# Three more pairs of the down projection in the seven-product form, their weight sums made during gate and up, and a written order for the loads

## The chip, the core and the metric

The kernel runs on one core of one Trainium2 chip. The metric is the device time of one execution in microseconds (us). TensorE (PE in the profile) multiplies matrices, VectorE (DVE) and ScalarE (ACT) work elementwise, GpSimd (POOL) here does little but issue transfers, and SyncE (SP) issues nearly all loads. Each engine takes its instructions in the order of its own queue. On-chip memory is named by tiles; a tile that is declared with `bufs=n` has n places that are used in turn, so whoever writes place k again waits for the last reader of what it held.

## What is computed

One decoder layer in float32 on 256 tokens of width 2048. The change lies in its last part:

```python
x = x + concat(PoolMixer, MLA, MemXAttn) @ W_o
h = rms_norm(x, g_ffn)
g = h @ w_gate                                   # 2048 x 5632
gc = conv_b + sum_j conv_w[j] * shifted(g, j)    # causal, width 3
x = x + (silu(gc) * (h @ w_up)) @ w_down         # w_down: 5632 x 2048
```

## The kernel before

**Precision.** Every float32 operand is split in two parts of a shorter type: a high part `wh` (ACT, `nc.scalar.copy`) and the rest `wl` (DVE, the operand minus its high part). A product takes three matmuls: high times high, low times high, high times low. `split_w` (L95) does this for weights. It writes into the tiles `wh` and `wl`, four places each of 128x1024, so at most four split blocks exist at a time.

**Gate and up** (loop at L879, 43 turns after the first). Turn f loads a block of 128x2048 of `w_g` and one of `w_u` into the staging tile `wr` (three places), splits each, and `gemm_pair` (L154) runs 96 matmuls with 256 columns. `glu` (L824) then makes 128 rows of the activation: convolution, SiLU, product, and its split. Two turns (f even, then odd) make one pair j of 256 rows; there are 22 pairs.

**Down** (loop at L988) goes twice over the 22 pairs, once for each half c of the output columns. For a pair and a half, the activation (256 tokens by 256 rows) and the weights (256 rows by 1024 columns, 1 MiB) are each seen as 2x2 blocks. Three kinds of pair exist; the string `KIND` (L43) has a letter for each place in `ORDER` (L42):

- `p`, plain (`plain`, L912): 8 block products, 24 matmuls with 512 columns. The weights are split in two pieces of 1024.
- `S` and `s`, seven products (`seven`, L940): 7 block products, 21 matmuls. They need sums of the blocks of the activation (seven blocks with high and low part: tile `aS`, made in `glu`, kept until down), and sums of the blocks of the weights. Split are one piece of 512 (`b11`) and three of 1024 (`b2`, then `t13` and `t24` from the sums).
- For `s`, DVE makes the weight sums in down (`make_sums`, L928), ahead of the pair: the instructions stand in the middle of the pair before it, where `seven` and `plain` call `between`. For `S`, they were made ahead of time: `presum` (L859) runs in odd turns of gate and up, loads the block through the same staging tile `wr`, makes four subtractions of 128x512 on DVE, and writes 1 MiB to a tensor in device memory, `tsum`. In down, `seven` then loads 0.75 MiB of the block and 1 MiB of `tsum`.

Before, 14 of 22 pairs take seven products; 8 of these are `S`, so 16 sums are made in gate and up.

**What sets the order.** A scheduler orders each engine's queue by what it expects to be ready, except for instructions marked by `keep` (L91), which stay in the order in which they are written. In down nearly everything on ACT, DVE and PE is kept; in gate and up nothing is, the loads on SP included. Loads of down (`load_dn`, L897) use four places in turn: three of `wr` and one in the tile `dn`.

Of the kernel before, what the change touches and what calls it, by code (L numbers as in the profile page):

```python
# [18 lines left out]
P = 128  # L19
# [22 lines left out]
ORDER = tuple(range(PAIRS - 3)) + (PAIRS - 1, PAIRS - 2, PAIRS - 3)  # L42
KIND = "pSspSsSpsSpSspSsSpsSpp"  # L43
# [20 lines left out]
def layer(ctx, tc, xT_d, xn_d, memT_d, vec_d, tab_d, w_z_d, w_mqkr_d, w_q_d, w_kv_d, w_mem_d, w_pool_d, w_o_d,  # L64
# [759 lines left out]
    def glu(f, psg, psu, home=None):  # L824
# [34 lines left out]
    def presum(i):  # L859

        raw = load_w(w_dn_d[SUMMED[i]], STG)
        r = raw.rearrange("p (b n) -> p b n", n=NN)
        for d, a, b in ((0, 1, 0), (1, 2, 1), (2, 2, 0), (3, 3, 2)):
            nc.vector.tensor_tensor(r[:, d], r[:, a], r[:, b], op=ALU.subtract)  # L864
# [30 lines left out]
    cnt = [0, 0]  # L895

    def load_dn(src, parts=((0, STG),)):  # L897

        cnt[1] += 1
        raw = dn[:, 4:8].rearrange("p b n -> p (b n)") if cnt[1] % 4 == 0 else stage.tile(  # L900
            [P, STG], F32, tag="wr", name=nm("wr"), bufs=3)[:]
        for a, b in parts:
            nc.sync.dma_start(raw[:, a:b], src[:, a:b])
        return raw
# [7 lines left out]
    def plain(c, j, own, first, last, kept, between=None, by_bank=False):  # L912
# [8 lines left out]
        for k, t, n in order:  # L921
            a = [aT[j][:, k, o + t * P:o + (t + 1) * P] for o in (0, T)]
            s = n if k == 0 else 1 - n
            prod(own[t, n], a, [w[:, s * NN:(s + 1) * NN] for w in ws[k]], first and k == 0, last and k == 1)

    ready = {}

    def make_sums(c, j):  # L928

        raw = load_dn(w_dn_d[c, j])  # L930
        r3 = raw.rearrange("p (b n) -> p b n", n=NN)
        i = cnt[0] % 2
        cnt[0] += 1
        f13, f24 = dn[:, 2 * i:2 * i + 2], dn[:, 2 - 2 * i:4 - 2 * i]
        keep(nc.vector.tensor_tensor(f13, r3[:, 1:3], r3[:, 0:2], op=ALU.subtract))
        keep(nc.vector.tensor_tensor(f24[:, 0], r3[:, 2], f13[:, 0], op=ALU.subtract))
        keep(nc.vector.tensor_tensor(f24[:, 1], r3[:, 3], f24[:, 0], op=ALU.subtract))
        ready[c, j] = (raw, *(f.rearrange("p b n -> p (b n)") for f in (f13, f24)))

    def seven(c, j, own, com, first, last, kept, between):  # L940
        if (c, j) in SUMMED:
            raw = load_dn(w_dn_d[c, j], ((0, NN), (2 * NN, STG)))
            sums = load_dn(tsum[:, SUMMED.index((c, j))])
            F13, F24 = sums[:, 0:HS], sums[:, HS:STG]
        else:
            raw, F13, F24 = ready.pop((c, j))
        b11 = split_w(raw, 0, NN, kept=kept)
# [3 lines left out]
        t13 = split_w(F13, 0, HS, kept=kept)  # L951
        t24 = split_w(F24, 0, HS, kept=kept)
        for (b, s), f, ps, own_ in (((b11, 0), 6, com[0], False), ((b2, 0), 5, own[0, 1], True),
                                    ((b2, 1), 0, own[0, 0], True), ((t13, 0), 2, com[1], False),
                                    ((t13, 1), 4, com[3], False), ((t24, 0), 3, com[2], False),
# [57 lines left out]
def _pack(**i):  # L1013
# [61 lines left out]
    w = np.stack([w[:, 0, :, :, 0], w[:, 0, :, :, 1], w[:, 1, :, :, 1], w[:, 1, :, :, 0]])  # L1075
# [19 lines left out]
```

## Time and profile before

| | |
|---|---|
| median of 3 runs | 996.81 us (996.54 to 997.71) |
| the profiled execution | 996.77 us, of which 994.8 us are its span |
| granted TensorE clock | 1.000 over the whole span |
| PE busy | 988.6 us |
| DVE busy / ACT busy | 756.8 us / 566.2 us |
| moved by DMA | 246.51 MB, mean 248 GB/s |
| gate and up, from the first of its matmuls at L165 | 301.7 to 769.8 us |
| down | 769.8 to 990.6 us |

The span runs from the first to the last instruction; the time of the execution has about 2 us around it. Busy shares are averages over stages with different limits. Matmuls overlap one another, so the length that the profile gives for one matmul is longer than the distance from its start to the next one's; distances between starts are what the PE queue costs.

### The profile page before, as it was taken

How to read it: one execution, taken by the hardware profiler on the slowest of the kernel's cores; microseconds unless marked ns; L12 is line 12 of the kernel's file. 1: busy time of each engine (PE TensorE's matmuls, PEld its weight loads, DVE VectorE, ACT ScalarE, POOL GpSimd, SP SyncE). 2: the span in 40 equal slices, each digit the busy share in tenths (PEclk: the TensorE clock that was granted, in tenths of full speed). 3: DMA queues.
4: the chain of work that ended last, by engine and by line, in shares of the span. 5: the costliest groups of instructions: out<-in, count | busy, mean ns of one | idle time of the engine just before them, and what ended most of it. 6: DMA issues, size and time to landing. Idle time of an engine off the chain costs nothing.

```text
span 994.8 us, 17144 instructions
## 1 busy us (share of the span) xinstructions
PE 988.6 (99%) x6888; PEld 916.3 (92%) x6888; DVE 756.8 (76%) x1117; ACT 566.2 (57%) x770; POOL 31.2 (3%) x63
## 2 busy tenths in 40 slices
PE   9999999999999999999999999999999999999998
PEld 7899988888889999999999999999999888888886
DVE  6878588765676777777787777876666988899897
ACT  6777666644565554554554455455544666746663
POOL 1100000000000000000000000000000000000000
PEclk9999999999999999999999999999999999999999
DMA  9867445344665888877788887775656887879772
GB/s 358 299 240 292 137 157 182 124 145 143 211 220 189 300 290 298 300 274 290 276 300 294 299 309 266 289 277 189 203 185 203 297 282 265 288 270 313 297 256 105
DMA packets 43808, 246.51 MB, mean 248 GB/s; under 512 B 4944, under 2 KB 5456, under 8 KB 19792
## 3 DMA queue, kind: packets, MB, share of 16 engines
q1 hardware_dynamic: 36576, 220.50, 63.1%
q0 software_dynamic: 6720, 24.12, 6.3%
q8 instruction: 54, 0.88, 0.3%
q10 hardware_dynamic: 432, 0.79, 0.3%
q14 instruction: 26, 0.21, 0.1%
HBM read 224.42 MB, written 20.97 MB: 247 GB/s over the span
## 4 chain that ended last, share of the span: by engine, by line
PE 96%; DVE 2%; DMA 1%; ACT 1%; issue 0%; DVEq 0%; ACTq 0%
PE psm L165 47%; PE psm L181 5%; PE psm L183 5%; PE psm L182 5%; PE psm L148 4%; PE psm L910 4%; PE psm L908 4%; PE psm L909 4%; PE psa L908 3%; PE psa L909 3%; PE psa L910 3%; PE psm L132 2%; PE psa L713 1%; PE psa L181 1%; PE psa L183 1%; PE psa L182 1%
## 5 line engine op out<-in xcount | busy, mean ns | idle before, releaser
L102 DVE TENSOR_TENSOR wl<-wr,wh 128x1024 fp32r<-128x1024 f32 (+2 forms) x362 | 419.1, 1168 | 166.9 <-ACT wh L101 110.1
L101 ACT CAST wh<-wr 128x1024 fp32r<-128x1024 f32 (+2 forms) x362 | 362.6, 1007 | 201.3 <-PE psm L165 84.7
L165 PE MATMUL psm<-h,wh 128*128 128x256 f32 x2752 | 319.1, 276 | 0.0
L165 PEld LDWEIGHTS psm<-h,wh 128*128 128x128 f32 x2752 | 315.3, 188 | 0.0
L165 PE MATMUL psm<-h,wl 128*128 128x256 f32 x1376 | 162.9, 276 | 0.0
L165 PEld LDWEIGHTS psm<-h,wl 128*128 128x128 f32 x1376 | 159.2, 188 | 0.0
L101 ACT CAST wh<-dn 128x1024 fp32r<-128x1024 f32 (+1 forms) x54 | 52.7, 976 | 32.2 <-PE psa L909 17.9
L102 DVE TENSOR_TENSOR wl<-dn,wh 128x1024 fp32r<-128x1024 f32 (+1 forms) x54 | 59.7, 1122 | 8.8 <-ACT wh L101 6.7
L828 ACT ACTIVATE gc<-g,vec 128x256 f32<-128x256 f32 x44 | 26.5, 603 | 70.0 <-DVE g L826 70.0
L831 ACT ACTIVATE gc<-gc 128x256 f32<-128x256 f32 x44 | 18.4, 419 | 70.5 <-DVE gc L830 70.4
L864 DVE TENSOR_TENSOR wr<-wr 128x512 f32<-128x512 f32 x64 | 44.0, 688 | 1.1
L830 DVE SCALAR_TENSOR_TENSOR gc<-g,vec,gc 128x255 f32<-128x255 f32 x88 | 42.2, 479 | 1.0
L910 PE MATMUL psm<-wl,aS 128*128 128x512 f32 x98 | 38.2, 390 | 0.1
L908 PE MATMUL psm<-wh,aS 128*128 128x512 f32 x98 | 38.1, 389 | 0.0
L910 PE MATMUL psa<-wl,aS 128*128 128x512 f32 x98 | 38.1, 389 | 0.0
L908 PE MATMUL psa<-wh,aS 128*128 128x512 f32 x98 | 38.1, 389 | 0.0
L909 PE MATMUL psa<-wh,aS 128*128 128x512 f32 x98 | 38.1, 389 | 0.0
L909 PE MATMUL psm<-wh,aS 128*128 128x512 f32 x98 | 38.1, 389 | 0.0
L181 PE MATMUL psm<-wh,cat 128*128 128x512 f32 x96 | 38.1, 397 | 0.0
L183 PE MATMUL psm<-wl,cat 128*128 128x512 f32 x96 | 37.4, 390 | 0.0
L182 PE MATMUL psm<-wh,cat 128*128 128x512 f32 x96 | 37.4, 389 | 0.0
L866 POOL DMA_DIRECT2D tsum<-wr x32 | 17.0, 533 | 344.5 <-DVE wr L864 344.5
(232 smaller groups left out, 1355.0 us busy)
## 6 DMA issues: line engine op xcount, KB each, us to landing
wr<-in_w_g SPq DMA_DIRECT2D x44, 1024.0 KB, 5.1
wr<-in_w_u SPq DMA_DIRECT2D x44, 1024.0 KB, 5.6
wr<-in_w_dn SPq DMA_DIRECT2D x37, 1024.0 KB, 5.0
wr<-in_w_o SPq DMA_DIRECT2D x16, 1024.0 KB, 4.9
tsum<-wr POOLq DMA_DIRECT2D x32, 512.0 KB, 4.1
wr<-tsum SPq DMA_DIRECT2D x12, 1024.0 KB, 6.2
wr<-in_w_z SPq DMA_DIRECT2D x10, 1024.0 KB, 6.8
dn<-in_w_dn SPq DMA_DIRECT2D x7, 1024.0 KB, 6.5
```

The source lines that it names most:

```text
L101: keep(nc.scalar.copy(hi[:, c:e], raw[:, o + c:o + e]), kept)
L102: keep(nc.vector.tensor_tensor(lo[:, c:e], raw[:, o + c:o + e], hi[:, c:e].bitcast(F32), op=ALU.subtract), kept)
L148: keep(nc.tensor.matmul(ps, parts[k // nk][low][:, i * P:(i + 1) * P], m, start=k + a == 0 and low == low_first, stop=k == KD - 1 and low ...
L165: nc.tensor.matmul(ps, parts[k // nk][low][:, i * P:(i + 1) * P], m, start=k + a == 0 and low == (s == 1), stop=k == KD - 1 and low == (s ...
L181: keep(nc.tensor.matmul(ps, xh, hi[:, i, o], start=first and i == 0, stop=False), kept)
L182: keep(nc.tensor.matmul(ps, xl, hi[:, i, o], start=False, stop=False), kept)
L183: keep(nc.tensor.matmul(ps, xh, lo[:, i, o], start=False, stop=last and i == nk - 1), kept)
L830: nc.vector.scalar_tensor_tensor(gc[:, d:T], g[:, 0:T - d], v(w, f), gc[:, d:T], op0=ALU.mult, op1=ALU.add)
L864: nc.vector.tensor_tensor(r[:, d], r[:, a], r[:, b], op=ALU.subtract)
L908: nc.tensor.matmul(ps, a[0], b[0], start=first, stop=False)
L909: nc.tensor.matmul(ps, a[1], b[0], start=False, stop=False)
L910: nc.tensor.matmul(ps, a[0], b[1], start=False, stop=last)
```

## The change

It does five things.

1. `KIND` and `ORDER`: 17 of 22 pairs take seven products, 14 of them as `S` (28 sums made in gate and up) and 3 as `s`.
2. The sums get their own staging tile `wj` with two places. Their loads (`job_load`) and the loads of gate and up are marked `keep`, so that SP's queue has them as written: after the two loads of a turn. The subtractions (`job_sums`) are written one turn later. A dictionary `job_at` spreads 28 jobs over the turns 2 to 41.
3. Five activations (`AWAY`, pairs 16 to 20) do not stay on the chip: they are written to `forms` in device memory and read back in each half of down into a single place `aL` (`fetch`, on POOL's queue, issued when the pair that used the place before is done).
4. In down the loads use six places in turn: three of `wr`, two of `wj`, one in `dn`.
5. The columns of the stored weight blocks are arranged so that an `S` pair's load is one transfer, and `make_sums` is four subtractions of 128x512 instead of one of 128x1024 and two of 128x512.

```diff
-ORDER = tuple(range(PAIRS - 3)) + (PAIRS - 1, PAIRS - 2, PAIRS - 3)
-KIND = "pSspSsSpsSpSspSsSpsSpp"
+KIND = "pSSSsSSpSSsSSpSsSSSSpp"
+ORDER = (0, 1, 16, 2, 3, 4, 17, 5, 21, 6, 18, 7, 8, 9, 19, 10, 11, 12, 20, 13, 14, 15)
+AWAY = (16, 17, 18, 19, 20)
...
-    def load_w(src, n, cut=STG):
+    def load_w(src, n, cut=STG, kept=False):
         raw = stage.tile([P, STG], F32, tag="wr", name=nm("wr"), bufs=3)
         for c in range(0, n, cut):
-            nc.sync.dma_start(raw[:, c:min(n, c + cut)], src[:, c:min(n, c + cut)])
+            keep(nc.sync.dma_start(raw[:, c:min(n, c + cut)], src[:, c:min(n, c + cut)]), kept)
...
-            aT[j] = home if j == PAIRS - 1 else fp.tile([P, 14, P], F32R, name=nm("aS"))[:]
+            aT[j] = (home if j == PAIRS - 1 else away() if j in AWAY
+                     else fp.tile([P, 14, P], F32R, name=nm("aS"))[:])
...
+            if j in AWAY:
+                nc.gpsimd.dma_start(forms[:, AWAY.index(j)], aT[j])
+    forms = dp.tile([P, len(AWAY), 14, P], F32R, name="forms")
+    def away():
+        return fp.tile([P, 14, P], F32R, tag="aL", name=nm("aL"), bufs=1)[:]
     tsum = dp.tile([P, len(SUMMED), STG], F32, name="tsum")
-    def presum(i):
-        raw = load_w(w_dn_d[SUMMED[i]], STG)
+    def job_place():
+        return fp.tile([P, STG], F32, tag="wj", name=nm("wj"), bufs=2)[:]
+    def job_load(i):
+        raw = job_place()
+        keep(nc.sync.dma_start(raw, w_dn_d[SUMMED[i]]))
+        return i, raw
+    def job_sums(i, raw):
         r = raw.rearrange("p (b n) -> p b n", n=NN)
-        for d, a, b in ((0, 1, 0), (1, 2, 1), (2, 2, 0), (3, 3, 2)):
+        for d, a, b in ((1, 0, 1), (0, 2, 0), (2, 2, 1), (3, 3, 2)):
             nc.vector.tensor_tensor(r[:, d], r[:, a], r[:, b], op=ALU.subtract)
...
+    job_at = {2 + i * (KF - 5) // (len(SUMMED) - 1): i for i in range(len(SUMMED))}
+    job = None
...
-        gemm_pair(pss, [load_w(w[f], STG) for w in (w_g_d, w_u_d)], h2)
+        gemm_pair(pss, [load_w(w[f], STG, kept=True) for w in (w_g_d, w_u_d)], h2)
         if f < KF - 1:
             glu(f, *pss)
-        if f % 2 and 3 <= f < 3 + 2 * len(SUMMED):
-            presum(f // 2 - 1)
+        if job is not None:
+            job_sums(*job)
+        job = job_load(job_at[f]) if f in job_at else None
...
-    def load_dn(src, parts=((0, STG),)):
-        cnt[1] += 1
-        raw = dn[:, 4:8].rearrange("p b n -> p (b n)") if cnt[1] % 4 == 0 else stage.tile(
-            [P, STG], F32, tag="wr", name=nm("wr"), bufs=3)[:]
-        for a, b in parts:
-            nc.sync.dma_start(raw[:, a:b], src[:, a:b])
+    def load_dn(src, a=0):
+        cnt[0] += 1
+        n = cnt[0] % 6
+        raw = (dn[:, 4:8].rearrange("p b n -> p (b n)") if n == 0 else job_place() if n % 3 == 1
+               else stage.tile([P, STG], F32, tag="wr", name=nm("wr"), bufs=3)[:])
+        nc.sync.dma_start(raw[:, a:STG], src[:, a:STG])
         return raw
...
+    def fetch(j):
+        aT[j] = away()
+        nc.gpsimd.dma_start(aT[j], forms[:, AWAY.index(j)])
...
     def make_sums(c, j):
         raw = load_dn(w_dn_d[c, j])
-        r3 = raw.rearrange("p (b n) -> p b n", n=NN)
-        i = cnt[0] % 2
-        cnt[0] += 1
-        f13, f24 = dn[:, 2 * i:2 * i + 2], dn[:, 2 - 2 * i:4 - 2 * i]
-        keep(nc.vector.tensor_tensor(f13, r3[:, 1:3], r3[:, 0:2], op=ALU.subtract))
-        keep(nc.vector.tensor_tensor(f24[:, 0], r3[:, 2], f13[:, 0], op=ALU.subtract))
-        keep(nc.vector.tensor_tensor(f24[:, 1], r3[:, 3], f24[:, 0], op=ALU.subtract))
-        ready[c, j] = (raw, *(f.rearrange("p b n -> p (b n)") for f in (f13, f24)))
+        r = raw.rearrange("p (b n) -> p b n", n=NN)
+        for d, a, b in ((1, r[:, 0], r[:, 1]), (0, r[:, 2], r[:, 0]), (2, r[:, 2], dn[:, 1]), (3, r[:, 3], dn[:, 2])):
+            keep(nc.vector.tensor_tensor(dn[:, d], a, b, op=ALU.subtract))
+        ready[c, j] = (raw, dn[:, 0:4].rearrange("p b n -> p (b n)"))
...
+        rest = [j for j in ORDER if j in AWAY]
+        fetch(rest.pop(0))
...
                 seven(c, j, own, com, j == SEVEN[0], j == SEVEN[-1], kept, between)
+                if j in AWAY and rest:
+                    fetch(rest.pop(0))
```

The letters stand under one another so:

```
before  pSspSsSpsSpSspSsSpsSpp
after   pSSSsSSpSSsSSpSsSSSSpp
```

**First place: DVE in down, the sums of an `s` pair.** DVE's queue before, at the sums for the pair at place 12 of the first half; `wl` with a `wh` is a split (512 wide: `b11`; then `b2`; after the sums `t13` and `t24`), `dn<-` are the sums. The pair at place 10, ahead of these rows' `S` pair, is plain: its two splits come first.

```order
L102 TENSOR_TENSOR wl_9202<-wr_9199,wh_9201 128x1024
L102 TENSOR_TENSOR wl_9206<-wr_9199,wh_9205 128x1024
L102 TENSOR_TENSOR wl_9238<-dn,wh_9237 128x512
L102 TENSOR_TENSOR wl_9242<-dn,wh_9241 128x1024
L935 TENSOR_TENSOR dn<-wr_9245 128x1024
L936 TENSOR_TENSOR dn<-wr_9245,dn 128x512
L937 TENSOR_TENSOR dn<-wr_9245,dn 128x512
L102 TENSOR_TENSOR wl_9251<-wr_9235,wh_9250 128x1024
L102 TENSOR_TENSOR wl_9255<-wr_9235,wh_9254 128x1024
```

DVE's queue of the change at the sums for the pair at place 10 of the first half:

```order
L103 TENSOR_TENSOR wl_9242<-wr_9237,wh_9241 128x512
L103 TENSOR_TENSOR wl_9246<-wr_9237,wh_9245 128x1024
L103 TENSOR_TENSOR wl_9250<-wr_9239,wh_9249 128x1024
L103 TENSOR_TENSOR wl_9254<-wr_9239,wh_9253 128x1024
L103 TENSOR_TENSOR wl_9283<-wj_9278,wh_9282 128x512
L103 TENSOR_TENSOR wl_9287<-wj_9278,wh_9286 128x1024
L959 TENSOR_TENSOR dn<-dn 128x512 x4
L103 TENSOR_TENSOR wl_9296<-wr_9280,wh_9295 128x1024
L103 TENSOR_TENSOR wl_9300<-wr_9280,wh_9299 128x1024
```

In both, the sums stand between `b2` and the first split of the sums; what has changed is the pair ahead: four splits of an `S` pair now, two of a plain pair before. It is so at places 4 and 10 of each half. At place 15 the `S` pair that carries the sums still follows a plain one.

**Second place: ACT at the start of gate and up.** ACT's queue before, from the square root of the normalization to the SiLU of turn 0 (`ACTIVATE gc<-gc`); `wh_3108` and `wh_3112` are the high parts of turn 1's `w_g`:

```order
L208 ACTIVATE rc<-rc,eps 128x2
L101 CAST wh_3108<-wr_3104 128x1024
L101 CAST wh_3112<-wr_3104 128x1024
L193 ACTIVATE h_2547<-psa_3002,vec 128x256
L193 ACTIVATE h_2547<-psa_3007,vec 128x256
L193 ACTIVATE h_2547<-psa_3012,vec 128x256
L193 ACTIVATE h_2547<-psa_3017,vec 128x256
L815 COPY r_2938<-psa_3028 128x256
L101 CAST wh_3164<-wr_3106 128x1024
L828 ACTIVATE gc_3093<-g_3091,vec 128x256
L101 CAST wh_3168<-wr_3106 128x1024
```

ACT's queue of the change from the same instruction:

```order
L209 ACTIVATE rc<-rc,eps 128x2
L194 ACTIVATE h_2547<-psa_3003,vec 128x256
L194 ACTIVATE h_2547<-psa_3008,vec 128x256
L194 ACTIVATE h_2547<-psa_3013,vec 128x256
L194 ACTIVATE h_2547<-psa_3018,vec 128x256
L816 COPY r_2938<-psa_3029 128x256
L829 ACTIVATE gc_3094<-g_3092,vec 128x256
L832 ACT_TABLE_LOAD
L832 ACTIVATE gc_3094<-gc_3094 128x256
L102 CAST wh_3109<-wr_3105 128x1024
L191 CAST aT_3099<-gc_3094 128x256
L102 CAST wh_3113<-wr_3105 128x1024
```

The casts of turn 1's `w_g` stand behind the SiLU of turn 0 now; on DVE the `wl` of the same block stands behind `glu`'s last product of turn 0 in the same way.

**Third place: SP in gate and up.** SP's queue of the change from turn 1 on:

```order
L89 DMA wr_3105<-in_w_g 128x2048
L89 DMA wr_3107<-in_w_u 128x2048
L89 DMA wr_3233<-in_w_g 128x2048
L89 DMA wr_3235<-in_w_u 128x2048
L874 DMA wj_3359<-in_w_dn 128x2048
L89 DMA wr_3363<-in_w_g 128x2048
L89 DMA wr_3365<-in_w_u 128x2048
L874 DMA wj_3499<-in_w_dn 128x2048
L89 DMA wr_3503<-in_w_g 128x2048
L89 DMA wr_3505<-in_w_u 128x2048
```

A load for sums stood in `wr` in every second turn before; it stands in `wj` in two of three turns now, with no place of `wr` taken.

More of the change, by code (lines that the diff above doesn't have):

```diff
@@ L922, in plain @@
             a = [aT[j][:, k, o + t * P:o + (t + 1) * P] for o in (0, T)]
-            s = n if k == 0 else 1 - n
+            s = 1 - n
             prod(own[t, n], a, [w[:, s * NN:(s + 1) * NN] for w in ws[k]], first and k == 0, last and k == 1)
+    def fetch(j):
+        aT[j] = away()
+        nc.gpsimd.dma_start(aT[j], forms[:, AWAY.index(j)])
     ready = {}
@@ L930, in make_sums @@
         raw = load_dn(w_dn_d[c, j])
-        r3 = raw.rearrange("p (b n) -> p b n", n=NN)
-        i = cnt[0] % 2
-        cnt[0] += 1
-        f13, f24 = dn[:, 2 * i:2 * i + 2], dn[:, 2 - 2 * i:4 - 2 * i]
-        keep(nc.vector.tensor_tensor(f13, r3[:, 1:3], r3[:, 0:2], op=ALU.subtract))
-        keep(nc.vector.tensor_tensor(f24[:, 0], r3[:, 2], f13[:, 0], op=ALU.subtract))
-        keep(nc.vector.tensor_tensor(f24[:, 1], r3[:, 3], f24[:, 0], op=ALU.subtract))
-        ready[c, j] = (raw, *(f.rearrange("p b n -> p (b n)") for f in (f13, f24)))
+        r = raw.rearrange("p (b n) -> p b n", n=NN)
+        for d, a, b in ((1, r[:, 0], r[:, 1]), (0, r[:, 2], r[:, 0]), (2, r[:, 2], dn[:, 1]), (3, r[:, 3], dn[:, 2])):
+            keep(nc.vector.tensor_tensor(dn[:, d], a, b, op=ALU.subtract))
+        ready[c, j] = (raw, dn[:, 0:4].rearrange("p b n -> p (b n)"))
     def seven(c, j, own, com, first, last, kept, between):
         if (c, j) in SUMMED:
-            raw = load_dn(w_dn_d[c, j], ((0, NN), (2 * NN, STG)))
+            raw = load_dn(w_dn_d[c, j], NN)
             sums = load_dn(tsum[:, SUMMED.index((c, j))])
-            F13, F24 = sums[:, 0:HS], sums[:, HS:STG]
         else:
-            raw, F13, F24 = ready.pop((c, j))
-        b11 = split_w(raw, 0, NN, kept=kept)
+            raw, sums = ready.pop((c, j))
+        b11 = split_w(raw, NN, NN, kept=kept)
         b2 = split_w(raw, 2 * NN, HS, kept=kept)
@@ L950, in seven @@
             between()
-        t13 = split_w(F13, 0, HS, kept=kept)
-        t24 = split_w(F24, 0, HS, kept=kept)
+        t31 = split_w(sums, 0, HS, kept=kept)
+        t24 = split_w(sums, HS, HS, kept=kept)
         for (b, s), f, ps, own_ in (((b11, 0), 6, com[0], False), ((b2, 0), 5, own[0, 1], True),
-                                    ((b2, 1), 0, own[0, 0], True), ((t13, 0), 2, com[1], False),
-                                    ((t13, 1), 4, com[3], False), ((t24, 0), 3, com[2], False),
+                                    ((b2, 1), 0, own[0, 0], True), ((t31, 1), 2, com[1], False),
+                                    ((t31, 0), 4, com[3], False), ((t24, 0), 3, com[2], False),
                                     ((t24, 1), 1, own[1, 0], True)):
@@ L1074, in _pack @@
     w = a["w_down"][0].reshape(PAIRS, 2, P, 2, 2, NN)
-    w = np.stack([w[:, 0, :, :, 0], w[:, 0, :, :, 1], w[:, 1, :, :, 1], w[:, 1, :, :, 0]])
+    w = np.stack([w[:, 0, :, :, 1], w[:, 0, :, :, 0], w[:, 1, :, :, 1], w[:, 1, :, :, 0]])
     r["w_dn"] = w.transpose(3, 1, 2, 0, 4).reshape(2, PAIRS, P, STG)
```

2 lines of the change are left out of this document (1 added, 1 removed).

## The prediction

> **What bounds the kernel now.** I read the page first: its busy times and its chain of waits.
>
> ```profile
> span 994.8 us, 17144 instructions
> PE 988.6 (99%) x6888; PEld 916.3 (92%) x6888; DVE 756.8 (76%) x1117; ACT 566.2 (57%) x770; POOL 31.2 (3%) x63
> PE 96%; DVE 2%; DMA 1%; ACT 1%; issue 0%; DVEq 0%; ACTq 0%
> ```
>
> PE is busy for 988.6 of 994.8 us, and the chain is PE's own queue for 96%. The 6 us left lie at the two ends, so no wait inside can be removed for a gain: only fewer matmuls make it faster, and every wait that is added on PE makes it longer. So two things are to be reckoned: the matmuls that go, and where PE starts to wait.
>
> What a matmul costs is read from the timeline of PE in down: the start of a plain pair (operand `aT`), of the seven-product pair behind it (`aS`), and of the pair after that.
>
> ```profile
> 804.31 0.39 PE L908 MATMUL psa<-wh,aT 128*128 128x512 f32 x1
> 809.75 0.39 PE L908 MATMUL psm<-wh,aS 128*128 128x512 f32 x1
> 814.51 0.39 PE L908 MATMUL psm<-wh,aS 128*128 128x512 f32 x1
> ```
>
> A plain pair takes 5.44 us for 24 matmuls, a seven-product pair 4.76 us for 21: 0.2267 us from start to start, back to back.
>
> **What goes: 4.1 us.** Three pairs change from plain to seven products, in two halves: 6 x 3 = 18 matmuls x 0.2267 = 4.08 us. Down becomes 954 x 0.2267 = 216.3 us.
>
> **What comes, 1: the sums of an `s` pair now meet full split buffers.** The next rows are ACT's, DVE's and PE's timeline: a seven-product pair that starts at 799.55, its split of `b2`, and then the one place of down where PE waits (827.48), with the sums ahead of it.
>
> ```profile
> 798.16 1.06 ACT L101 CAST wh<-wr 128x1024 fp32r<-128x1024 f32 x1 [0.30 <-PE psm L909]
> 797.89 2.59 DVE L102 TENSOR_TENSOR wl<-wr,wh 128x1024 fp32r<-128x1024 f32 x2 [0.21 <-ACT wh L101]
> 799.55 0.39 PE L908 MATMUL psm<-wh,aS 128*128 128x512 f32 x1
> ...
> 823.61 1.23 DVE L935 TENSOR_TENSOR dn<-wr 128x1024 f32<-128x1024 f32 x1 [2.06 <-DMA wr<-in_w_dn]
> 824.87 0.69 DVE L936 TENSOR_TENSOR dn<-wr,dn 128x512 f32<-128x512 f32 x1
> 825.60 0.69 DVE L937 TENSOR_TENSOR dn<-wr,dn 128x512 f32<-128x512 f32 x1
> 826.21 2.35 DVE L102 TENSOR_TENSOR wl<-wr,wh 128x1024 fp32r<-128x1024 f32 x2
> ...
> 826.97 0.39 PE L909 MATMUL psm<-wh,aS 128*128 128x512 f32 x1
> 827.48 0.50 PE L910 MATMUL psm<-wl,aS 128*128 128x512 f32 x1
> 827.82 0.40 PE L908 MATMUL psm<-wh,aS 128*128 128x512 f32 x1
> ...
> L910 PE MATMUL psm<-wl,aS 128*128 128x512 f32 x98 | 38.2, 390 | 0.1
> ```
>
> ACT's cast waits for PE (L909): the four places of `wh` are full, and a split can only be as far ahead as one seven-product pair. So in a row of such pairs the split of `b2` starts 1.66 us before its pair does (797.89 against 799.55). Another 1024-wide split may start 1.14 us later (two take 2.59 with a gap; 826.21 has two in 2.35, so 2.35 - 1.22 = 1.13). The first split of the sums is needed by the third matmul of its products, 9 + 2 = 11 matmuls or 2.49 us after the pair's start.
>
> Behind a plain pair there is more room: that pair has only two split tiles, so the next pair's `b2` finds its place a pair earlier. That is where all seven-product carriers of sums stand in the rows of before, and PE waits only once (the group's row has 0.1 us of idle time in all, the modelled ends hide the rest), where the sums' load was 2.06 us late. This one place shows the chain as it is: the split of 826.21 ends at 827.44, and the matmul that should have started at 827.20 starts at 827.48; the next starts at 827.82 instead of 827.43. That wait, 0.4 us, goes, as its pattern goes.
>
> At places 4 and 10 of each half the carrier now follows another seven-product pair. The time from the pair's start: `b2` at -1.66, sums from -0.52, 2.6 us (823.61 to 826.21; the new form, four of 512, has starts 0.6 to 0.73 apart, about the same), first split of the sums 2.08 to 3.31, where PE needs it at 2.49. That is 0.86 us, and 0.1 us is lost in starting again, as after 827.48. I take 0.9 us x 4 places = **3.7 us**. Below, it is nothing, if PE were a microsecond late there anyway; above, 2.6 us each, if nothing of the sums were hidden: 0 to 10 us. The third `s` pair, place 15, still sits behind a plain pair: nothing.
>
> **What comes, 2: the first turn of gate and up.** Rows of DVE, ACT and PE around 300 us:
>
> ```profile
> 298.36 1.10 PE L132 MATMUL psm<-h,wl 128*128 128x256 f32 x8
> 299.31 1.58 PE L132 MATMUL psm<-h,wh 128*128 128x256 f32 x12
> 300.72 1.10 PE L132 MATMUL psm<-h,wl 128*128 128x256 f32 x8
> 301.66 0.28 PE L165 MATMUL psm<-h,wh 128*128 128x256 f32 x1
> ...
> 299.56 0.42 DVE L826 TENSOR_TENSOR g<-psm,r 128x256 f32<-128x256 f32 x1 [1.68 <-issue]
> 300.02 0.60 ACT L828 ACTIVATE gc<-g,vec 128x256 f32<-128x256 f32 x1 [0.37 <-DVE g L826]
> 302.11 1.28 ACT L831 ACT_TABLE_LOAD   x1
> 303.41 0.42 ACT L831 ACTIVATE gc<-gc 128x256 f32<-128x256 f32 x1
> 303.74 1.05 ACT L101 CAST wh<-wr 128x1024 fp32r<-128x1024 f32 x1
> ```
>
> Turn 1's first matmul (301.66) needs a cast which ACT now does behind turn 0's SiLU. From the start of `g`: 0.46 to the convolution's first step, 0.60 for it, 1.28 table load (it covers DVE's two steps of 0.48), 0.33 SiLU to the next start, 1.05 cast: 3.72 us, and 0.25 from gate's last matmul (next start 299.31) to `g` (299.56): 4.0 us. PE has turn 0's up to do meanwhile, 24 matmuls at (301.66 - 299.31)/20 = 0.118: 2.8 us. It waits 1.2 us; some 0.2 us come back, since the reordering lets `h2` be ready earlier. **1.0 us**; at most 2.4 (no cover by the reordered part, and `wl` late too), at least 0.
>
> **What comes, 3: work beside PE.** Twelve more sums in gate and up: 12 x 4 subtractions of 0.69 us, and 12 x 2.1 MB; five forms out (4.6 MB). In down per half: 8 loads of 1.05 MB, 14 of 1.835 MB, five forms of 0.92 MB, 1.05 MB of `x1s`: 39.7 MB, and 80.5 MB for both with the output of the first half; by the same count 61.9 MB before. The rows of five windows (the last two numbers are DMA share and GB/s), then the sums' group, their stores' landing, SP's first load of down, and gate and up in the chain:
>
> ```profile
> 320.00:660.00 340.00, 340.00 (x3003) 340.00 (x3002) 260.17 (x379) 173.14 (x207) 17.04 (x32) 1.00 0.81 291
> 775.00:860.00 85.00, 84.88 (x374) 69.91 (x374) 76.86 (x77) 55.02 (x59) 0.00 (x0) 1.00 0.81 277
> 10.00:30.00 20.00, 20.00 (x90) 16.57 (x89) 16.44 (x24) 15.67 (x25) 1.22 (x2) 1.00 1.03 413
> 890.00:900.00 10.00, 10.00 (x46) 8.29 (x45) 8.20 (x8) 5.91 (x7) 0.00 (x0) 1.00 1.03 371
> 815.00:826.00 11.00, 11.00 (x50) 9.13 (x49) 8.07 (x9) 6.60 (x8) 0.00 (x0) 1.00 0.97 354
> ...
> L864 DVE TENSOR_TENSOR wr<-wr 128x512 f32<-128x512 f32 x64 | 44.0, 688 | 1.1
> tsum<-wr POOLq DMA_DIRECT2D x32, 512.0 KB, 4.1
> 750.37 5.77 SPq L903 DMA_DIRECT2D wr<-in_w_dn  x3
> 301.82 467.93 PE psm L165 x4128
> ```
>
> In gate and up DVE is at 260/340 = 77%; 33 us more over 468 us make it 84% at most. DMA moves 291 GB/s there; with two jobs in three turns it is 10.5 MB in 3 x 10.88 us (467.93 over 43 turns) = 321 GB/s, against 413 over 10 to 30 us. Each load of `wr` has three half turns (16 us) from the release of its place to its use, so I cost this at nothing. SP's new waits: a sums' load waits for the store of the job two before, made at least three half turns earlier with 4.1 us to land; the next `w_g` load queued behind it isn't held up. POOL's queue: the fetch waits for PE's last use of `aL`, has three pairs (14.3 us) to land, and only later fetches and the first half's output queue behind it. Nothing again; the price if the cover is gone is the lateness itself.
>
> In down the cover is thin; that is the first rival.
>
> **Sum.** 996.77 - 4.1 - 0.4 + 3.7 + 1.0 = **997.0 us**, from the profiled execution (span 994.8 and 2 us around it; the median 996.81 is the same to 0.04).
>
> **Rivals.**
>
> *Loads late in down: slower.* PE's time to the start of the last seven-product pair is 216.3 - 2 x 5.44 - 4.76 = 200.7 us, and 3.7 of waits less 3 for the splits: 201 us. By then all but 2.1 MB (two plain pairs) and some 5.6 MB that arrive ahead of down (three pairs and a form; before, SP issues down's first load at 750) must land: 72.8 MB, **362 GB/s**. This is the point from which it decides. The first rows say 413 is possible, but in down itself the two stretches with always a load waiting give 371 and 354. At 354: 72.8/0.354 = 205.6, so 4.6 us more, 1001.6 us; at 340, 13 us more. For it: DVE already waits 2.06 us for a load in down at 277 GB/s. Against it: that wait came with four places, and there are six now. The Trainium skill ("SBUF — State Buffer", "Summary: rules for kernel authors") tells one to reckon transfers between device memory and SBUF at about 358 GB/s; as an estimate, 72.8 MB then take 203.4 us, 2.4 us more than PE leaves. The 413 GB/s row disagrees, and "HBM Reference", "Specifications (TRN2)", of the same skill has a core streaming alone above that share, as the row does.
>
> *PE does not wait at places 4 and 10: faster.* Then 3.7 us stay: 993.3 us; without the wait at turn 1 as well, 992.3. For it: eleven of twelve places of sums made PE wait for nothing before. Against: none of them followed a seven-product pair.
>
> *Gate and up get waits of their own* (321 GB/s, two jobs in consecutive turns: 8.4 MB in 21.8 us, 385 GB/s for a while): slower, 999 to 1003 us. Three half turns of lead speak against it.
>
> **Chances.** What a measurement of this kernel can tell from no change is about 0.2%, 2 us. The forecast, waits of 4 to 5 us that eat the matmuls' gain, has 0.50, with its own range 994.8 to 998.8; the faster rival 0.20; late loads 0.25; gate and up 0.05. So faster 0.20, same 0.50, slower 0.30. The range takes in the faster rival with both waits gone (992.4) and late loads down to about 352 GB/s (1002.5); 0.1 is left out above, a little below.
>
> **What would show it.** Right: 21 matmuls per pair in 17 pairs, PE in down near 216 us plus gaps; at places 4 and 10 a gap of about 0.9 us at L931, the third matmul of the first product with sums, with a split by DVE ending just before; a gap of about 1 us ahead of turn 1's first matmul, released by ACT's cast. Wrong: SP or DVE waiting for loads in down with the DMA share at 1 for tens of us (late loads), no gaps at L931 (the faster rival), or PE idle in the middle of gate and up.

## The result, and where the time went

The changed kernel takes **1011.74 us** (median of 4 runs, 1009.83 to 1016.98); the kernel before 996.85 us beside it. The ratio is 1.0156, 95% interval 1.0118 to 1.0195: slower. The prediction was 997.0 us, in a range of 992.4 to 1002.5: it was wrong.

The profiled execution took 1012.18 us. First the page's own lines: span, busy times and the chain of waits by engine, and the start of the chain by line.

```profile
span 1010.4 us, 17323 instructions
PE 993.7 (98%) x6870; PEld 917.5 (91%) x6870; DVE 785.0 (78%) x1174; ACT 567.5 (56%) x779; POOL 52.1 (5%) x102
PE 66%; DVE 14%; DMA 14%; issue 3%; ACT 3%; SPq 0%; DVEq 0%; ACTq 0%
PE psm L166 17%; DMA wj<-in_w_dn 9%; DVE wl L103 8%; PE psm L182 5%; PE psm L184 5%; PE psm L183 5%; PE psm L149 4%; PE psa L931 4%; PE psm L931 4%; PE psa L930 4%; PE psa L929 4%; PE psm L930 4%; PE psm L929 4%; DMA tsum<-wj 2%; PE psm L133 2%
```

PE still looks 98% busy, but the chain is no longer its own queue: 96% became 66%, and the load of a job's block (`wj<-in_w_dn`) and DVE's splits came in. Two windows tell which stage it is: gate and up from the first matmul of turn 1, and down (after the x-count: granted clock, DMA share, GB/s).

```profile
303.92:788.60 484.68, 476.42 (x4129) 0.99 0.88 325
788.60:1005.75 217.15, 217.15 (x954) 1.00 0.90 342
```

| | before | after | difference |
|---|---|---|---|
| first matmul of turn 1 | 301.66 | 303.92 | +2.26 |
| gate and up, turns 1 to 43 | 467.93 | 484.68 | +16.75 |
| down, to the end of the span | 225.2 | 221.8 | -3.4 |
| span | 994.8 | 1010.4 | +15.6 |

(Before, gate and up end at 301.66 + 467.93 = 769.6.) So the change gains in down, loses a little at the start, and loses 16.8 us in gate and up, where PE had no wait before. By the distances between the starts of matmuls, 10.6 of the 16.8 us are gaps of more than 0.25 us, 2.7 us are smaller ones, and 3.4 us come from two stretches of 3.41 us in which PE ran at half its clock. One of these stretches follows the gap ahead of turn 1 (last section): its 1.7 us belong to the start, and about **15.1 us** to what happens further on. Three views show by what. PE's waits (us in total, times, the longest):

```profile
PE psm L166 <- DVE wl L103: 8.1, 10, 2.2
PE psm L166 <- ACT wh L102: 2.1, 1, 2.1
```

The group of the jobs' sums on DVE (busy us and mean ns, then the idle time ahead of them and what ended most of it):

```profile
L881 DVE TENSOR_TENSOR wj<-wj 128x512 f32<-128x512 f32 x112 | 77.1, 688 | 56.0 <-DMA wj<-in_w_dn 54.5
```

And the DMA issues (KB each, median us from issue to landing):

```profile
wr<-in_w_g SPq DMA_DIRECT2D x44, 1024.0 KB, 7.3
wr<-in_w_u SPq DMA_DIRECT2D x44, 1024.0 KB, 5.4
wj<-in_w_dn SPq DMA_DIRECT2D x32, 1024.0 KB, 8.7
tsum<-wj POOLq DMA_DIRECT2D x56, 512.0 KB, 7.8
```

PE waits for splits that DVE makes (the 8.1 us recorded are less than what was lost, since the modelled ends of matmuls hide part of a gap; distances between starts are what counts). DVE itself stands for 54.5 us ahead of the sums of L881, because their block has not landed. Before, the sums' group had 1.1 us of idle time. Two such places in the timelines of SP, DVE and PE; the first:

```profile
332.21 0.33 SPq L874 DMA_DIRECT2D wj<-in_w_dn  x1
332.63 0.53 SPq L89 DMA_DIRECT2D wr<-in_w_g  x1
334.93 0.33 SPq L89 DMA_DIRECT2D wr<-in_w_u  x1
...
334.82 0.48 DVE L831 SCALAR_TENSOR_TENSOR gc<-g,vec,gc 128x255 f32<-128x255 f32 x1
339.60 0.69 DVE L881 TENSOR_TENSOR wj<-wj 128x512 f32<-128x512 f32 x1 [4.30 <-DMA wj<-in_w_dn]
340.21 0.48 DVE L831 SCALAR_TENSOR_TENSOR gc<-g,vec,gc 128x254 f32<-128x254 f32 x1
340.61 2.14 DVE L881 TENSOR_TENSOR wj<-wj 128x512 f32<-128x512 f32 x3
342.66 1.22 DVE L103 TENSOR_TENSOR wl<-wr,wh 128x1024 fp32r<-128x1024 f32 x1
344.46 1.22 DVE L103 TENSOR_TENSOR wl<-wr,wh 128x1024 fp32r<-128x1024 f32 x1
...
345.73 1.19 PE L166 MATMUL psm<-h,wl 128*128 128x256 f32 x8 [0.59 <-DVE wl L103]
```

SP issues the job's load at 332.21, and the sums start 7.4 us later. DVE comes to the sums at 335.3 and waits until 339.60. In its queue the splits of the next half turn stand behind the sums (a half turn is the work on one block of 128x2048: two splits and 48 matmuls, 5.44 us); the second of them ends at 345.7, and PE has run out of work by then. In this place SP itself was late: it issued the load 7.9 us after the one before it in its queue (324.33), having waited for a place of `wj`. At 13 of the 15 places where DVE waits, SP issues the load at once, as here:

```profile
428.22 0.33 SPq L89 DMA_DIRECT2D wr<-in_w_u  x1
428.65 0.37 SPq L874 DMA_DIRECT2D wj<-in_w_dn  x1
...
432.62 1.22 DVE L103 TENSOR_TENSOR wl<-wr,wh 128x1024 fp32r<-128x1024 f32 x1
437.60 0.69 DVE L881 TENSOR_TENSOR wj<-wj 128x512 f32<-128x512 f32 x1 [3.44 <-DMA wj<-in_w_dn]
438.21 1.22 DVE L103 TENSOR_TENSOR wl<-wr,wh 128x1024 fp32r<-128x1024 f32 x1
...
445.05 1.21 PE L166 MATMUL psm<-h,wl 128*128 128x256 f32 x8 [0.90 <-DVE wl L103]
```

DVE comes to these sums 5.5 us after the load was issued; the block needs 8.8 us. That is a reading of a trace; the experiments are to tell whether it is the cause.

### The profile page after: what moved, and what is told of

The parts are those of the page before. It is cut to its first block, busy times and chain, and to the rows that moved or that the text cites. A ratio compares the mean times of both kernels' runs of the same rounds, so it can differ in the third digit from the quotient of the medians.

```text
span 1010.4 us, 17323 instructions
## 1 busy us (share of the span) xinstructions
PE 993.7 (98%) x6870; PEld 917.5 (91%) x6870; DVE 785.0 (78%) x1174; ACT 567.5 (56%) x779; POOL 52.1 (5%) x102
## 4 chain that ended last, share of the span: by engine, by line
PE 66%; DVE 14%; DMA 14%; issue 3%; ACT 3%; SPq 0%; DVEq 0%; ACTq 0%
PE psm L166 17%; DMA wj<-in_w_dn 9%; DVE wl L103 8%; PE psm L182 5%; PE psm L184 5%; PE psm L183 5%; PE psm L149 4%; PE psa L931 4%; PE psm L931 4%; PE psa L930 4%; PE psa L929 4%; PE psm L930 4%; PE psm L929 4%; DMA tsum<-wj 2%; PE psm L133 2%
## 5 line engine op out<-in xcount | busy, mean ns | idle before, releaser
L103 DVE TENSOR_TENSOR wl<-wr,wh 128x1024 fp32r<-128x1024 f32 (+2 forms) x344 | 396.5, 1162 | 97.4 <-ACT wh L102 91.2
L102 ACT CAST wh<-wr 128x1024 fp32r<-128x1024 f32 (+2 forms) x344 | 336.0, 1000 | 130.1 <-PE psm L183 49.3
L881 DVE TENSOR_TENSOR wj<-wj 128x512 f32<-128x512 f32 x112 | 77.1, 688 | 56.0 <-DMA wj<-in_w_dn 54.5
L102 ACT CAST wh<-wj 128x1024 fp32r<-128x1024 f32 (+1 forms) x48 | 47.1, 982 | 22.1 <-PE psa L930 11.6
L103 DVE TENSOR_TENSOR wl<-wj,wh 128x1024 fp32r<-128x1024 f32 (+1 forms) x48 | 53.7, 1133 | 6.3 <-ACT wh L102 2.4
L883 POOL DMA_DIRECT2D tsum<-wj x56 | 29.9, 534 | 398.8 <-DVE wj L881 335.4
L103 DVE TENSOR_TENSOR wl<-dn,wh 128x1024 fp32r<-128x1024 f32 (+1 forms) x36 | 40.1, 1133 | 3.4 <-ACT wh L102 1.7
L102 ACT CAST wh<-dn 128x1024 fp32r<-128x1024 f32 (+1 forms) x36 | 35.3, 982 | 10.7 <-PE psa L930 4.9
L929 PE MATMUL psa<-wh,aS 128*128 128x512 f32 x84 | 32.7, 389 | 0.0
L930 PE MATMUL psm<-wh,aS 128*128 128x512 f32 x84 | 32.7, 389 | 0.0
L930 PE MATMUL psa<-wh,aS 128*128 128x512 f32 x84 | 32.7, 389 | 0.0
L929 PE MATMUL psm<-wh,aS 128*128 128x512 f32 x84 | 32.7, 389 | 0.0
```

Source lines behind the costliest of these rows:

```text
L102: keep(nc.scalar.copy(hi[:, c:e], raw[:, o + c:o + e]), kept)
L103: keep(nc.vector.tensor_tensor(lo[:, c:e], raw[:, o + c:o + e], hi[:, c:e].bitcast(F32), op=ALU.subtract), kept)
L929: nc.tensor.matmul(ps, a[0], b[0], start=first, stop=False)
L930: nc.tensor.matmul(ps, a[1], b[0], start=False, stop=False)
```

## The experiments

**Theory A**: DVE's queue stands still behind sums whose block has not landed, and the splits behind come late. **Theory B**: gate and up moves too many bytes (325 GB/s against 265 before), so loads are late. **Theory C**: DVE has too much work. Each ratio below is against the kernel before, run on the same chip.

**e1: no subtractions in gate and up.** The S pairs of down then multiply unsummed blocks; all bytes still move.

```diff
 def job_sums(i, raw):
-        for d, a, b in ((1, 0, 1), (0, 2, 0), (2, 2, 1), (3, 3, 2)):
-            nc.vector.tensor_tensor(r[:, d], r[:, a], r[:, b], op=ALU.subtract)
```

> The changed kernel without the 112 subtractions of the 28 jobs in gate and up: the blocks are loaded and written back to tsum as they are, so every byte still moves, and the S pairs of down multiply the blocks themselves in place of their sums. Theory A (DVE's queue stands still behind sums whose block has not landed, and the splits behind them come late): gate and up go back from 484.7 to about 468 us, the time to 994 to 996.5 us. Theory B (loads of gate and up are themselves late, since DMA moves 325 GB/s there): nothing changes, 1009 to 1013 us. Theory C (DVE has too much work, wherever its sums stand): as A, 994 to 996.5 us; C and A are told apart by the next kernel.

Measured: 995.97 us, ratio 0.9992 (0.9983 to 1.0002). Gate and up last 468.0 us, as before the change, with the bytes of the change: theory B falls. A and C are left.

**e2: the same sums, two or three half turns later in DVE's queue.** `gemm_pair` calls `between`, which is `job_sums` of the last turn's job, behind the splits of gate's block, and the sums are pinned there.

```diff
-            nc.vector.tensor_tensor(r[:, d], r[:, a], r[:, b], op=ALU.subtract)
+            keep(nc.vector.tensor_tensor(r[:, d], r[:, a], r[:, b], op=ALU.subtract))
...
             parts = [split_w(raw, c * HS, HS, shift=16 if c else 48) for c in range(KD // nk)]
+            if between is not None and s == 0:
+                between()
```

> The changed kernel with the same loads, sums and stores, but the sums pinned in DVE's queue behind the splits of gate's block of the turn after their load, two half turns later than they stand now; all that is computed stays. Theory A: DVE no longer waits for the blocks (54.5 us of such waits before), gate and up take 468 to 472 us, the time is 994 to 1000 us; some of the gain may go again where jobs stand in three turns in a row, since SP then waits for a place of wj longer. Theories B and C: as many bytes and as much work, so 1009 to 1013 us.

Measured: 997.2 us, ratio 0.9997 (0.9987 to 1.0006). The window of gate and up:

```profile
303.69:771.80 468.11, 468.11 (x4129) 1.00 0.91 336
```

The group of the sums:

```profile
L883 DVE TENSOR_TENSOR wj<-wj 128x512 f32<-128x512 f32 x112 | 77.1, 688 | 1.9
```

The issues of the blocks' loads:

```profile
wj<-in_w_dn SPq DMA_DIRECT2D x32, 1024.0 KB, 7.6
```

The sums have the same 77.1 us of work, the bytes are the same and move faster (336 GB/s), and the blocks take nearly as long to land; yet DVE's wait ahead of the sums is gone (54.5 us; now the group idles 1.9 us in all), and with it the loss in gate and up. (This execution has no half clock behind the gap ahead of turn 1, which is the other 1.7 of the 16.8 us.) So **A is shown**, and neither the bytes nor the work are the cause. SP waited longer for places of `wj` (64.0 us in all, 10.5 in the changed kernel), which never reached PE.

**e3: 16 jobs in place of 28.** Six S pairs become plain (36 more matmuls in down, 8.2 us).

```diff
-KIND = "pSSSsSSpSSsSSpSsSSSSpp"
+KIND = "pSSpspSpSpsSppSsSpSppp"
```

> The changed kernel with six of the S pairs made plain, so that 16 jobs instead of 28 are spread over gate and up, as many as before the change, with its new places and order; down has 36 more matmuls (8.2 us). Theory A: what counts is where sums stand behind their load, not how many there are: waits of DVE at its jobs stay, gate and up lose about 16/28 of 16.8 us, 9 to 10 us, less where a lone job finds SP's queue less full (4 us at the least): 472 to 478 us for gate and up. Theory B: 16 jobs are as many bytes as before the change, so 468 us. Theory C: 468 to 469 us.

Measured: 1003.86 us, ratio 1.0071 (1.0056 to 1.0086); gate and up 467.9 us. A's number was wrong here: PE lost nothing. DVE did wait for blocks, but less:

```profile
DVE wj L881 <- DMA wj<-in_w_dn: 23.8, 10, 5.1
```

10 waits of 2.4 us, against 15 of 3.6 us, disappeared in DVE's free time. The loss is not proportional to the jobs. It fits that it begins where DVE's slack ends, since with 28 jobs DVE has both more waits and less slack; no run varies the slack alone.

**e8: the job's load written ahead of its turn's loads** in place of behind them; the sums unpinned where they were.

```diff
+        last, job = job, job_load(job_at[f]) if f in job_at else None
         gemm_pair(pss, [load_w(w[f], STG, kept=True) for w in (w_g_d, w_u_d)], h2)
...
-        if job is not None:
-            job_sums(*job)
-        job = job_load(job_at[f]) if f in job_at else None
+        if last is not None:
+            job_sums(*last)
```

> The changed kernel with each job's load written ahead of the two loads of its turn in place of behind them, 10.9 us earlier; the sums are written where they were, unpinned. If what counts is where the load stands in SP's queue, the blocks land in time: gate and up 468 to 472 us, 994 to 999 us. If what counts is how far behind its load the sums stand in DVE's queue, nothing is won, since the order by the expected time of landing moves the sums along with the load (one job's load stands behind that of half turn 11, its sums behind the split of half turn 10; they were behind 13 and 12): 1008 to 1014 us.

Measured: 1010.23 us, ratio 1.0139 (1.0123 to 1.0154), and DVE waits as before the move:

```profile
DVE wj L881 <- DMA wj<-in_w_dn: 52.6, 15, 5.0
```

An earlier load does not help, since the sums are unpinned and move up with it. The traces show it job by job: how long after the issue of its load DVE reaches a job's first subtraction, and how long the block takes to land.

| | jobs | DVE reaches the sums after | block lands after | DVE waits |
|---|---|---|---|---|
| before | 16 | 5.3 to 5.7 us | 4.7 to 5.2 us | nowhere |
| after, those with a wait | 15 | 3.1 to 5.9 us | 7.0 to 10.7 us | at all 15 |
| after, the others | 13 | 10.2 to 11.6 us | 6.7 to 9.6 us | nowhere |
| e8, those with a wait | 15 | 4.5 to 5.9 us | 6.9 to 10.4 us | at all 15 |
| e8, the others | 13 | 7.0 to 12.3 us | 4.8 to 10.7 us | nowhere |
| e2 | 28 | 13.5 to 21.9 us | 4.8 to 10.8 us | nowhere |

So what counts is the distance between the two in the queues, against the time to landing. In the changed kernel the unpinned sums stand one half turn behind the issue of their load in 14 of the 15 places with a wait (in the 15th, 332.21, SP was late), and two or more in the 13 others. Where DVE does not wait, it reaches the sums after the landing, job by job.

**e4: the start alone.** The splits of turn 1's gate block are written ahead of `glu(0)`, whose first steps are pinned behind them.

```diff
+    raws = [load_w(w[1], STG, kept=True) for w in (w_g_d, w_u_d)]
+    split1 = halves(raws[0])
     glu(0, *pss)
```

> The changed kernel with the splits of turn 1's gate block written ahead of glu of turn 0 on ACT and DVE, as they stood before the change; all else stays. If the start of gate and up costs PE's wait (2.3 us) and in addition the lower granted clock behind it (32 matmuls in 5.37 us instead of 3.71, that is 1.7 us), 3.9 us go: about 1008 us. If the clock is lower there for another reason than the wait, 2.2 us go: 1009.6 us. If the waits further on take up what is won (DVE is late for other reasons anyway), nothing goes: 1011.7 us.

Measured: 1011.05 us (1008.9 to 1014.72), ratio 1.0156 (1.0136 to 1.0175). Turn 1 starts at 301.7 again, but the times of this kernel and of the changed one spread over 6 to 7 us, so the gain cannot be read here. It is read from the next kernel, where nothing else disturbs.

**e5: e2 and e4 together.**

> The sums later (as in the second kernel) and the splits of turn 1's gate block ahead of glu of turn 0 (as in the fourth), both in one. The two losses are apart, so both gains add: gate and up start at 301.7 us and take 468 us. The second kernel's times lie in two groups, near 995.5 and near 997.3 us. If the 1.8 us between them are the lower clock that follows the 2.1 us gap ahead of turn 1 in some executions, the new times lie in one group at 993.3 to 993.9 us, 3.0 us under the kernel before. If the lower clock has nothing to do with that gap, there are still two groups, 993.4 and 995.2 us. If the fix of the start is worth as little here as it was alone (0.7 us), 996.5 us.

Measured: 993.59 us (993.48 to 993.66), ratio 0.9963 (0.9950 to 0.9975). That is 3.6 us under e2 (the kernel before took 996.87 and 996.93 us beside them), where the start moved by 2.2 us only (303.69 to 301.52). Seven of e2's ten times lie between 996.83 and 997.47 us, one at 996.16 and two at 995.40 and 995.55; e5's five lie within 0.2 us. So the gap ahead of turn 1 costs its 2 us, and in most executions up to 1.8 us more (last section); e2's profiled execution, 995.40 us, is one without it.

**e6: the sums of `s` pairs behind plain pairs.** As many pairs of each kind as in e5.

```diff
-KIND = "pSSSsSSpSSsSSpSsSSSSpp"
+KIND = "pSsSSSSpSsSSSpSsSSSSpp"
```

> The kernel of e5 with KIND changed so that each s pair's sums are made in a seven-product pair that follows a plain pair (s at places 2, 9 and 15 in place of 4, 10 and 15); as many pairs of each kind. If the sums at places 4 and 10 make PE wait 0.9 us each, as predicted, 3.7 us go: 989.8 us. If PE hardly waits there (starts of its matmuls in down leave 1.0 us over 957 x 0.2267 us in all), at most 0.8 us go: 992.6 to 993.6 us.

Measured: 992.61 us, ratio 0.9953 (0.9940 to 0.9965): 1.0 us less than e5, not 3.7. (Down has 954 matmuls, not 957; their starts leave 1.2 us over 954 x 0.2267 in e5, and 0.1 us in e6.)

**e7: the products' matmuls pinned**, on e5.

```diff
 def prod(ps, a, b, first, last):
-        nc.tensor.matmul(ps, a[0], b[0], start=first, stop=False)
+        keep(nc.tensor.matmul(ps, a[0], b[0], start=first, stop=False))
...
```

> The kernel of e5 with the matmuls of the products in down pinned in the order in which they are written; nothing else. In the trace of the changed kernel PE runs the high-part matmuls of the following products ahead of the low-part matmul that lacks its split (806.78 us), at the four places where the sums follow a seven-product pair, and nearly nowhere else. Theory 1 (this reordering is what hid the predicted waits): now the third matmul of the first product with sums waits 0.7 to 0.9 us at each of four places; 2.2 to 3.6 us more than e5. Theory 2 (the split is in time, or the matmul queue absorbs it): within 0.5 us of e5.

Measured: 1000.18 us, ratio 1.0031 (1.0021 to 1.0042), 6.6 us more than e5. The first of the four places, DVE above and PE below:

```profile
784.34 1.29 DVE L966 TENSOR_TENSOR dn<-wr 128x512 f32<-128x512 f32 x2
785.54 1.41 DVE L966 TENSOR_TENSOR dn<-wr,dn 128x512 f32<-128x512 f32 x2
786.87 2.35 DVE L103 TENSOR_TENSOR wl<-wj,wh 128x1024 fp32r<-128x1024 f32 x2
...
787.12 0.39 PE L937 MATMUL psm<-wh,aS 128*128 128x512 f32 x1
788.14 0.50 PE L938 MATMUL psm<-wl,aS 128*128 128x512 f32 x1 [0.63 <-DVE wl L103]
788.48 0.39 PE L936 MATMUL psm<-wh,aS 128*128 128x512 f32 x1
```

From 787.12 to 788.14 is 1.02 us where 0.227 is the rule: 0.80 us lost, and the same 0.80 at each of the other three places (817.29, 899.09, 929.26); 0.11 us more goes to the next start (788.48). That is the prediction's wait of 0.9 us, which the changed kernel does not have. There, at the same place, PE's queue reads:

```profile
805.53 0.39 PE L929 MATMUL psm<-wh,aS 128*128 128x512 f32 x1
805.76 0.39 PE L930 MATMUL psm<-wh,aS 128*128 128x512 f32 x1
805.99 0.39 PE L929 MATMUL psm<-wh,aS 128*128 128x512 f32 x1
806.21 0.39 PE L930 MATMUL psm<-wh,aS 128*128 128x512 f32 x1
806.44 0.39 PE L929 MATMUL psm<-wh,aS 128*128 128x512 f32 x1
806.78 0.73 PE L931 MATMUL psm<-wl,aS 128*128 128x512 f32 x2
```

Instead of waiting at 805.99 for the low part, PE runs three more high-part matmuls (L929, L930 of the next products), and 0.11 us is left of the wait, ahead of each of the two low-part matmuls at 806.78: 0.9 us over the four places, which is what e6 won. In e7 the four places cost 3.6 us, and 3.9 us are lost in the same way in the plain pairs at the end of each half (1.39 us at 875.81, 1.35 at 987.83 and smaller ones), where the unpinned kernel reorders too; the expectation did not have these.

**e9: four places for the loads of down**, on e6.

```diff
-        n = cnt[0] % 6
-        raw = (dn[:, 4:8].rearrange("p b n -> p (b n)") if n == 0 else job_place() if n % 3 == 1
+        n = cnt[0] % 4
+        raw = (dn[:, 4:8].rearrange("p b n -> p (b n)") if n == 0
                else stage.tile([P, STG], F32, tag="wr", name=nm("wr"), bufs=3)[:])
```

> The kernel of e6 with four places for the loads of down, as before the change (three of wr, one in dn), in place of six. Theory 1 (the two places of wj are what keeps loads from coming late in down, where 80.5 MB must pass in 217 us): DVE and ACT wait for loads at L103 and PE behind them; with the 354 GB/s of the stretch of before where a load was always waiting, 4 to 5 us more: 996.5 to 998 us. Theory 2 (the transfers are hidden with four places too, places matter little): 992.4 to 993.2 us.

Measured: 1005.09 us, ratio 1.0082 (1.0065 to 1.0100): 12.5 us more than e6, over twice what was expected. The longest groups of waits for loads in down:

```profile
ACT wh L102 <- DMA wr<-in_w_dn: 18.2, 11, 3.7
ACT wh L102 <- DMA wr<-tsum: 9.9, 7, 2.1
```

Two windows of 10 us (busy PE, PEld, DVE, ACT, POOL, then clock, DMA share, GB/s):

```profile
840.00:850.00 10.00, 10.00 (x46) 8.28 (x45) 9.53 (x12) 7.66 (x9) 0.53 (x1) 1.00 0.76 267
...
900.00:910.00 10.00, 8.48 (x35) 5.78 (x34) 4.55 (x6) 4.54 (x6) 0.00 (x0) 1.00 1.03 417
```

Loads come late although DMA is not always busy: at 840 it has time left (0.76, 267 GB/s), because no place is free (SP issues nothing from 838.64 to 845.36 and waits 6.3 us of it for a split to free one), and at 900 it works at 417 GB/s and PE waits. With six places the transfers even out: in e6 the windows of 10 us from 770 to 970 all have a DMA share of 0.83 or more, 373 GB/s from 770 to 971 against 354 here, and no load is waited for. So it is the places, more than a mean rate, that keep loads in time.

**e10: no three jobs in a row**, on e6.

```diff
-    job_at = {2 + i * (KF - 5) // (len(SUMMED) - 1): i for i in range(len(SUMMED))}
+    job_at = {1 + i // 2 * 3 + i % 2: i for i in range(len(SUMMED))}
```

> The kernel of e6 with the 28 jobs in two of every three turns, turns 1, 2, 4, 5 to 40, 41, in place of a spread that has three turns with a job in a row at times. In e6 SP waits 61.9 us in all for a place of wj (17 times, the longest 8.4 us) with the loads of gate and up queued behind it. If those waits reach PE, 0.5 us or more go; if the loads' lead of three half turns swallows them, the time is that of e6, 992.4 to 992.8 us.

Measured: 992.32 us (992.16 to 992.45), ratio 0.9946 (0.9932 to 0.9961). SP's waits for a place of `wj` fall from 61.9 to 42.3 us. Against e6 the step is 0.3 us, and the two intervals overlap: a gain is not shown. e5, e6 and e10 beat both kernels; e6 and e10 are 0.5% below the kernel before and 1.9% below the changed one.

## Why the prediction was wrong

**What goes (4.1 us): right.** In the profiled execution down fell by 3.4 us, with about 1 us of new waits in it.

**Comes 3 (work beside PE, costed at nothing): this is the step that failed.** It looked at DVE's busy share, at DMA's rate and at SP's and POOL's waits. Of DVE it counted the work of twelve more jobs, but not the wait that sums bring into an in-order queue when their block has not landed. That wait cost about 15.1 us. "Each load of `wr` has three half turns" is true of the splits' loads; the job's block has its own, shorter lead. A job's load goes out behind that of half turn L, which waits for the split of L - 3; at 14 of the 15 places with a wait, the sums stand behind the split of L - 2, one half turn on. In the kernel before one half turn was enough, since a block landed in 4.7 to 5.2 us; now it lands in 7.0 to 10.7 us at these places, and DVE arrives 3.1 to 5.9 us after the issue. The prediction reckoned with neither the distance nor the new landing time. Before, a job's load was issued 5.9 us behind the load ahead of it and 5 us ahead of the next; now it mostly goes out 0.43 us behind the load ahead of it. With only 16 jobs, as many as before, e3 has landings of 6.7 to 10.3 us too, so the number of jobs is not the reason; that the close neighbour is the reason was not tested by itself. The claim that SP would not be held up by a place of `wj` failed too, three times for 10.5 us in all, 332.21 among them.

The rival "gate and up get waits of their own" had the right place, but its mechanism was the rate (385 GB/s for a while) and its price 2 to 6 us, not 15; e1 and e2 show that the rate is not what decides.

**Comes 2 (the start, 1.0 us): right in place and releaser, too small.** The gap was 2.3 us (the last eight matmuls of turn 0 start at 300.68, so PE is free at 300.68 + 8 x 0.118 = 301.62). The working let the table load cover DVE's two convolution steps; but ACT waits for them first:

```profile
301.22 1.28 ACT L832 ACT_TABLE_LOAD   x1 [1.11 <-DVE gc L831]
```

That is the 1.1 us that the sum lacks. And the half clock behind the gap, 1.7 us more in the profiled execution, was no term of the sum.

**Comes 1 (3.7 us in down): the chain was right, the result was not.** The prediction had the sums 0.52 us ahead of the pair; they start at 802.97 for a pair that starts at 803.49, exactly that. e7 has the wait at 0.80 and 0.11 us, where 0.86 and 0.1 were reckoned. What failed is the assumption that PE takes its matmuls as written. In down the splits and sums are pinned, the matmuls of `prod` are not, before the change or after it ("nearly everything on ACT, DVE and PE is kept" is not so for PE's products), and the queue that results has the high-part matmuls moved ahead at just these four places. So about 1.0 us remained of 3.7 (e6). The order's rows of PE would have shown it.

**Late loads in down (0.25): did not come.** The forecast's condition, 362 GB/s, was met without a wait for a load: from 788.6 us on, 201 us of down ran at 369 GB/s. So the row of 354 GB/s by which the rival was reckoned was no ceiling, and the estimate of 203.4 us for these bytes was too long. e9 shows that the six places are the reason, as the prediction argued against this rival.

With comes 2 and comes 3 taken away, as e5 does, and comes 1 at the measured 1.0 us, the sum gives 996.8 - 4.1 - 0.4 + 1.0 = 993.3 us; e5 has 993.59.

## What to carry to other kernels

When work that waits for a transfer is put into an engine's in-order queue, its price is not its busy time but the lateness of its transfer at the moment the engine reaches it; compare the distance between load and consumer in that queue with the landing time, and look at what stands behind the consumer. If a load and its consumer are ordered by an expected time of landing, pin the consumer: moving the load alone moves both (e8). And before a wait is reckoned on an engine, read in the order itself whether its queue is the written one; unpinned matmuls filled most of each 0.8 us wait here.

## What the runs showed of the hardware beside this

A short gap of PE can cost more than its length. The granted clock in windows of one microsecond of the changed kernel, behind the gap of 2.1 us ahead of turn 1:

```profile
303.00:304.00 1.00, 0.08 (x1) 1.00 0.00 0
304.00:305.00 1.00, 1.00 (x8) 0.88 0.00 0
305.00:306.00 1.00, 1.00 (x7) 0.50 0.00 0
306.00:307.00 1.00, 1.00 (x6) 0.50 0.00 0
307.00:308.00 1.00, 1.00 (x7) 0.50 0.57 74
308.00:309.00 1.00, 1.00 (x10) 0.92 0.58 221
```

The clock falls to half about a microsecond after PE has gone on, for some 3.4 us; the 32 matmuls there take 5.37 us instead of 3.71 (e2). The same followed the gap ahead of turn 1 in e8, a gap of 2.20 us at 635 in this kernel, one of 2.90 us in e4, and two of 0.93 and 0.62 us within 2.4 us in e8 (at 476). It does not come each time: two gaps of 1.40 and 0.58 us in e4 (at 443) were followed by nothing, and the profiled executions of e1, e2 and e3 have the gap of 2.1 us ahead of turn 1 with the clock at 1.00 behind it.

The times at which the traces record a change of the clock explain most of this. Each such half clock lasts 3.41 us, and the full clock between two of them a whole multiple of that (327.68 us is 96 x 3.413, in e8 170.67 us is 50 x 3.413). So the clock changes on a fixed raster. What decides seems to be how much of PE's idle time falls into one window of the raster: in the five cases with a half clock the window just before it holds 1.55 to 2.65 us of idle time. In e2 and e3 a boundary cuts the gap (1.02 and 1.12 us, 0.88 and 1.27), and the two gaps of e4 lie in different windows (1.40 and 0.58); no half clock follows. One case does not fit: e1 has 1.75 us in one window and keeps the full clock.

It fits e2's times, most of which lie near 995.5 or near 997.2, and e5's, which has no gap and one group. The mean clock recorded for each execution bears it out: a half clock of 3.41 us lowers the mean over 994 us by 0.0017, and it is 0.998 in the six of e2's ten executions that took 997.16 us or more, 0.999 or 1.000 in the four others; e1 has 0.998 in its three above 997.3 and 0.999 or 1.000 in its seven up to 996.14. The Trainium skill ("TensorE: Matmul & The Clock Gate", "Part 1: The HAM clock gate") says that the clock is halved after an idle window of about 3.4 us that runs freely, and returns after as long a busy one. The length of the half clock and its coming and going agree with that, and so does the raster; the gaps here were shorter than its window.
